# More products ahead of one head's last values and of another's third scores, and one unit's sums of weights tied behind the unit's addition

## The chip, the cores and the metric

The kernel runs on one core of one Trainium2 chip. Its time is the device time of one execution in microseconds, and lower is better. Three executions of the kernel before took 969.65, 969.67 and 970.43 us.

The profile's names for the engines are PE (TensorE's matmuls), PEld (TensorE's weight loads, which overlap the matmuls), DVE (VectorE), ACT (ScalarE), POOL (GpSimd) and SP (SyncE, which issues the loads of weights here).

## The reference, cut to what matters

The program is a decoder trunk of two layers over 512 tokens and 16 learned meta tokens, 1024 wide: first a gated linear attention, then a differential softmax attention with eight heads. All that the change touches lies in the second layer, and in that layer's projections:

```python
def diff_branch(xn, w_in, lam_vecs, gnorm, w_out, rel_table, lambda_init):
    proj = xn @ w_in
    q, k, v, z = jnp.split(proj, 4, axis=-1)
    ...
        s = jnp.einsum('bhpqd,bhpkd->bhpqk', qb, kh) * scale + bias[None, :, None]
        s = jnp.where(dist >= 0, s, -jnp.inf)
        p = jax.nn.softmax(s, axis=-1)
        a = p[:, :, 0] - lam * p[:, :, 1]
        return jnp.einsum('bhqk,bhkv->bhqv', a, vh)
    ...
    o = head_rms(o) * gnorm.astype(f32) * (1.0 - lambda_init)
    y = jax.nn.silu(z.astype(f32)) * o.reshape(B, L, D_INNER)
    return (y.astype(xn.dtype) @ w_out)
```

A head has two maps of scores, whose softmaxes are subtracted (`a`), values of 256 columns, a normalisation over them, a gate z, and its share of the output product.

## The kernel before, in words

**Exactness.** Every float32 operand of a matmul is split into a high and a low part (`split`, lines 284 and 285: ScalarE writes the high part, VectorE subtracts it from the source for the low part). A product is the sum of three matmul passes: high times high, high times low, low times high. In the profile `wh` and `wl` are the two parts of a block of weights, `a11h` and `a11l` those of one block, `aT` a head's turned weights of attention.

**Projections.** q, k, v and z of each head come from blocks of 256 columns of `w_in`. Each is a `Unit`: seven products of blocks instead of eight, with sums of weight blocks made ahead of them (`want_unit`, its function `sums` with three additions on VectorE, line 375; its block of raw weights comes by DMA, tile `raw`, and the sums go to the tile `sum`) and combinations of results after them (`add` in `Unit.run`, lines 493 to 497, which leaves its last instruction in `W.mark`). The banks of results are `bx`, `by` and `bv`. The q of heads 0 and 1 is a plain product of 512 columns instead (line 430, in `project`). A unit's column is its `c0`: q of head hd has c0 = 256 hd, so c0 = 768 is the q of head 3, whose weights are prepared while head 2 runs.

**What sets the order.** TensorE's instructions go in the order in which the program writes them. `W` (a `Weaver`) holds a queue of projections for the next head; between two steps of a head's attention, `W.fill(us)` takes so many microseconds of products off the queue, by a table of costs, and writes them there. VectorE's and ScalarE's instructions are ordered by a scheduler that knows priorities and dependences; `issue_after(x)` ties what stands in it behind the instruction x.

**A head's attention** (`diff_steps`) runs over four blocks of queries, the largest first. A step A makes the scores and the exponentials of a block (matmuls line 409, `ps<-k,q`; the shortest rows and sums on VectorE, line 1733; the exponential on ScalarE, line 1735), B turns the weights (lines 1757 and 1758, tiles `aT` and `am`), C makes the values (matmuls line 409, `ps<-v,aT`, and one short matmul, line 1773, `ps<-vm,am`) and normalises them: ScalarE, lines 1777 and 1778, a power on GpSimd, line 1780, and ScalarE again, line 1781, tile `on`. E turns two normalised blocks (line 1789, `ps<-ident,on`) and multiplies by z (VectorE, line 1792). The order of the steps with the number of the block is

```python
steps = [(A, 0), (A, 1), (B, 0), (A, 2), (C, 0), (B, 1), (A, 3), (C, 1), (B, 2), (E, 1), (C, 2), (B, 3),
         (C, 3), (E, 3)]
steps = [(f, o[i]) for f, i in steps]
```

with o = (3, 2, 1, 0), so `(C, 3)` makes the values of block 0. After each step stands a fill, whose least size depends on the step: 0 after A, 2.4 after B and C, 1.0 after E.

**The last head** keeps only the first six steps. The rest is written out after the loop, mixed with `final_rows`, the closing product with `w_out` (line 1863, `bx<-x,hT`). In this head lines 891 and 892 turn blocks of v (tiles `y` and `vm`; on VectorE lines 285 and 421), and lines 1589 to 1591 make the gate z.

Of the kernel before, what the change touches and what calls it, by code (L numbers as in the profile page):

```python
# [217 lines left out]
def trunk(ctx, tc, x, meta, g_norm, gla_w_in, gla_w_gate_up, gla_b_gate, gla_gnorm, gla_w_out,  # L218
# [9 lines left out]
    d_w_in, d_lam, d_gn, d_w_out = diff_w_in[0], diff_lam[0], diff_gnorm[0], diff_w_out[0]  # L228
# [85 lines left out]
    def in_rows(t):  # L314
        return t.rearrange("p (k c) -> p k c", c=P)
# [49 lines left out]
    def want_unit(w, c0, calm=False):  # L365
        def single(tag, b):
            def fn(raw):
                t = [T(wp, [P, 512], F32R, tag + part, bufs=1) for part in "hl"]
                with tc.issue_after(W.moved.ins) if calm and b == 0 else ExitStack():
                    split(*[in_rows(o) for o in t], block(raw, b))  # L370
                return t
            return Part(tag, fn)

        def add(o, a, b):
            dve.tensor_tensor(o, a, b, op=ALU.add)

        def sums(raw):
            t = T(wp, [P, 2, 512], F32, "sum", bufs=1)
            add(in_rows(t[:, 1, :]), block(raw, 2), block(raw, 3))
            add(in_rows(t[:, 0, :]), in_rows(t[:, 1, :]), block(raw, 0))  # L380
            add(block(raw, 2), block(raw, 2), block(raw, 0))
            return t

        def outer(raw):
            add(block(raw, 0), block(raw, 1), in_rows(su.t[:, 0, :]))
            ws.room["sum"] += 1
            return block_pair(raw[:, :4, :])

        a11, a12, a22 = single("a11", 0), single("a12", 1), single("a22", 3)
        su = Part("sum", sums)  # L390
        s21 = Part("pair", lambda raw: block_pair(su.t))
        s43 = Part("pair", outer)
        ws.want((w, c0), [a11, su, s21, a12, s43, a22])
        return a11, a12, a22, s21, s43
# [1510 lines left out]
    for hd in range(D_HEADS):  # L1905
        last = hd == D_HEADS - 1
        s = heads[hd]
        W.finish(projs[hd])
        W.settle()
        for chain in ready:  # L1910
            W.follow(*chain)
        ready.clear()
        s.scored, s.begun = False, True
        out2 = None
        keep = {D_HEADS - 1: 0.0, D_HEADS - 2: 22.0}.get(hd, 3.0)
        if 2 <= hd < D_HEADS - 1:
            pair = hd - 2 - hd % 2
            out2 = q_diff_out2(pair, ys[pair:pair + 2], range(2) if hd == D_HEADS - 2 else [hd % 2])
        if not last:
            n = heads[hd + 1]  # L1920
            late = hd == D_HEADS - 2
            if not late:
                gates.append(q_diff_z(hd + 1, n))
                values.append(q_diff_v(hd + 1, n))
            W.stop = q_diff_k(hd + 1, n)
            projs.append(q_diff_q(hd + 1, n))
            if late:
                values.append(q_diff_v(hd + 1, n))
                gates.append(q_diff_z(hd + 1, n))
        if hd == D_HEADS - 2:  # L1930
            ws.room["none"] = 0
            wt = want_last(hd)

            def freed():
                ws.room["none"] += 2
                ws.pump()
            gates[-1].freed = freed
        (A, B, C, E), o = diff_steps(hd, s, ys), (3, 2, 1, 0)
# [3 lines that stand above are left out]
        share = {A: 1.5, B: 1.1, C: 1.1, E: 0.5}  # L1942
        if last:
            steps = steps[:6]
        W.fill(4.0)
        for n, (f, b) in enumerate(steps):
            if last and n == 4:
                if values[hd] in W.queue:
                    W.finish(values[hd])
                W.settle()  # L1950
                W.fill(2.0)
            if n == 4:
                W.land()
            if n == 5 and gates[hd] in W.queue:
                W.finish(gates[hd])
            if last and n == 5:
                gfin = T(xp, [P, D], F32, "x0", bufs=1)
                sp.dma_start(gfin, g_final.partition_broadcast(P))
            if n == 5:
                if out2 in W.queue:  # L1960
                    W.finish(out2)
                ys.append([yt[hd % 3][:, i] for i in range(2)])
            f(b)
            if f is A and b == 0:
                s.scored, W.stop = True, None
                if not last:
                    heads[hd + 1].T = bias_tile(hd + 1)
            W.fill(max((W.left - keep) * share[f] / sum(share[g] for g, _ in steps[n:]),
                       ((4.0, 3.0, 5.2, 3.0, 4.6, 3.0, 4.0, 3.0)[hd]) if n == len(steps) - 2 else {A: 0.0, B: 2.4, C: 2.4, E: 1.0}[f]))
    W.finish()  # L1970
    W.settle()
    ws.pump()
# [53 lines left out]
```

## Time and profile before

| | |
|---|---|
| median of three runs | 969.67 us |
| profiled execution | 971.08 us |
| its span, first to last instruction | 968.4 us |
| mean granted TensorE clock | 0.996 |
| TensorE matmuls busy | 953.0 us, 98% of the span |
| VectorE busy | 798.2 us, 82% |
| ScalarE busy | 635.6 us, 66% |
| GpSimd busy | 81.3 us, 8% |

The first layer fills the span up to about 460 us. The first scores of head 0 stand at 501 us, those of head 1 at 555, of head 2 at 606, of head 3 at 668 and of the last head at 912. A row of the timeline gives start, busy time, engine, line, operation, tiles, and in brackets how long the engine had been idle and what released it. Several like instructions in a row are drawn together (x7), and their time is then the whole of it.

### The profile page before, as it was taken

To read this page: it belongs to the slowest core of one execution; us is meant where nothing else is said; L and a number is where in the kernel's file an instruction comes from. 1 tells how busy PE (TensorE), PEld (TensorE's weight loads), DVE (VectorE), ACT (ScalarE), POOL (GpSimd) and SP (SyncE) were. 2 spreads that over 40 slices of the span, in tenths; PEclk is the share of its full clock that TensorE was granted. 3 is DMA by queue.
4 is the path that set the end of the run, shared out by engine and by line. 5 is a ranking of instruction groups with operands and counts; after the bars stand their busy time and mean duration, and the time that the engine had idled before them with its cause. 6 is when DMAs were issued, how large, how long until landed. Compare 5 with 4: busy or idle time off the path is not lost.

```text
span 968.4 us, 18488 instructions
## 1 busy us (share of the span) xinstructions
PE 953.0 (98%) x7173; PEld 912.4 (94%) x7173; DVE 798.2 (82%) x1557; ACT 635.6 (66%) x1313; POOL 81.3 (8%) x164
## 2 busy tenths in 40 slices
PE   9999999999999999999999999999999999999997
PEld 8999999999999999998899898999999999989986
DVE  7989886886878787667997887879879889888875
ACT  7776755477647567656757685576766766755673
POOL 1000000000000000000001121111101101110111
PEclk9999999999999999999999999999999999999999
DMA  8322223635462237134356515234252261533312
GB/s 197 88 79 61 86 72 126 142 109 119 123 164 89 87 112 162 47 107 152 99 133 152 127 56 142 83 123 113 87 149 87 80 159 44 145 91 98 110 44 87
DMA packets 128602, 104.96 MB, mean 108 GB/s; under 512 B 51181, under 2 KB 112909, under 8 KB 128512
## 3 DMA queue, kind: packets, MB, share of 16 engines
q1 hardware_dynamic: 123184, 93.80, 35.3%
q10 hardware_dynamic: 5328, 9.95, 2.8%
q8 instruction: 57, 0.93, 0.4%
q14 instruction: 33, 0.27, 0.1%
HBM read 83.64 MB, written 11.80 MB: 99 GB/s over the span
## 4 chain that ended last, share of the span: by engine, by line
PE 73%; DVE 8%; ACT 4%; DMA 3%; issue 2%; POOL 1%; SPq 0%; POOLq 0%; DVEq 0%; ACTq 0%
PE bx L440 17%; PE bv L440 10%; PE by L440 9%; PE ps L409 7%; PE bx L997 5%; PE bx L430 4%; PE bx L409 3%; DMA raw<-in_diff_w_in_dram 3%; PE bv L997 2%; PE by L997 2%; PE ps L1239 2%; PE bv L409 1%; PE by L409 1%; DVE wl L285 1%; PE ps L1863 1%
## 5 line engine op out<-in xcount | busy, mean ns | idle before, releaser
L285 DVE TENSOR_TENSOR wl<-raw,wh 128x1024 fp32r<-128x1024 f32 x93 | 113.5, 1221 | 20.5 <-ACT wh L284 20.0
L284 ACT ACTIVATE wh<-raw 128x1024 fp32r<-128x1024 f32 x93 | 97.9, 1053 | 45.2 <-PE by L997 23.2
L440 PE MATMUL bv<-x,wh 128*128 128x264 f32 (+1 forms) x736 | 108.9, 285 | 0.1
L440 PE MATMUL bx<-x,wh 128*128 128x264 f32 (+1 forms) x720 | 105.6, 285 | 0.4 <-ACT ps L1777 0.4
L440 PEld LDWEIGHTS bv<-x,wh 128*128 128x128 f32 x736 | 96.8, 188 | 0.9 <-DVE z L497 0.3
L440 PEld LDWEIGHTS bx<-x,wh 128*128 128x128 f32 x720 | 94.4, 188 | 1.1 <-ACT ps L1777 0.7
L285 DVE TENSOR_TENSOR wl<-sum,wh 128x1024 fp32r<-128x1024 f32 x46 | 56.2, 1221 | 11.6 <-ACT wh L284 11.2
L461 ACT ACTIVATE u<-bx 128x264 f32<-128x264 f32 (+1 forms) x128 | 48.4, 378 | 21.8 <-PE bx L440 18.9
L440 PE MATMUL bv<-x,wl 128*128 128x264 f32 (+1 forms) x368 | 62.2, 286 | 0.1
L1735 ACT ACTIVATE p<-p,st 128x528 f32<-128x528 f32 (+3 forms) x64 | 36.4, 569 | 38.7 <-DVE st L1733 38.5
L440 PE MATMUL bx<-x,wl 128*128 128x264 f32 (+1 forms) x360 | 59.2, 284 | 0.0
L284 ACT ACTIVATE wh<-sum 128x1024 fp32r<-128x1024 f32 x46 | 48.4, 1051 | 10.4 <-PE bv L440 6.3
L440 PE MATMUL by<-x,a12h 128*128 128x264 f32 (+1 forms) x360 | 52.6, 285 | 0.9 <-DVE t L495 0.9
L440 PE MATMUL bx<-x,a11h 128*128 128x264 f32 (+1 forms) x360 | 53.0, 285 | 0.0
L440 PEld LDWEIGHTS bv<-x,wl 128*128 128x128 f32 x368 | 51.4, 188 | 0.4 <-issue 0.3
L284 ACT ACTIVATE a11h<-raw 128x512 fp32r<-128x512 f32 x46 | 28.9, 627 | 33.3 <-DMA raw<-in_diff_w_in_dram 12.8
L440 PEld LDWEIGHTS bx<-x,wl 128*128 128x128 f32 x360 | 50.0, 188 | 0.6 <-DVE wl L285 0.4
L440 PEld LDWEIGHTS bx<-x,a11h 128*128 128x128 f32 x360 | 47.8, 189 | 0.6
L440 PEld LDWEIGHTS by<-x,a12h 128*128 128x128 f32 x360 | 46.9, 188 | 1.1 <-DVE t L495 1.1
L565 POOL TENSOR_TENSOR st<-st,mhalf 128x1 f32<-128x1 f32 (+1 forms) x20 | 12.1, 606 | 386.5 <-DVE st L564 386.5
L1738 POOL TENSOR_TENSOR st<-st,minus 128x1 f32<-128x1 f32 x32 | 21.1, 658 | 279.4 <-ACT p L1735 226.4
L440 PE MATMUL by<-x,a22h 128*128 128x264 f32 (+1 forms) x280 | 40.1, 284 | 0.0
(501 smaller groups left out, 2671.8 us busy)
## 6 DMA issues: line engine op xcount, KB each, us to landing
raw<-in_diff_w_in_dram SPq DMA_DIRECT2D x52, 512.0 KB, 5.0
raw<-in_gla_w_in_dram SPq DMA_DIRECT2D x48, 512.0 KB, 4.5
raw<-in_gla_w_out_dram SPq DMA_DIRECT2D x8, 1024.0 KB, 6.0
raw<-in_diff_w_out_dram SPq DMA_DIRECT2D x8, 1024.0 KB, 5.3
raw<-in_diff_w_in_dram SPq DMA_DIRECT2D x6, 1024.0 KB, 6.0
vd<-planes ACTq DMA_DIRECT2D x12, 268.0 KB, 4.3
vd<-keep ACTq DMA_DIRECT2D x12, 264.0 KB, 2.3
T<-bdr SPq DMA_DIRECT2D x8, 264.0 KB, 3.8
```

Source lines behind the costliest of these rows:

```text
L284: act.activation(hi, src, AF.Copy)
L285: dve.tensor_tensor(lo, src, hi.bitcast(F32), op=ALU.subtract)
L409: pe.matmul(ps, l, r, start=first and n == 0, stop=last and n == 2, **kw)
L430: pe.matmul(bank, a[:, k, :], b[k] if n0 is None else b[k][:, n0 + i * nn:n0 + (i + 1) * nn], start=n == 0 and ks[0] == 0, stop=n == len(t ...
L440: pe.matmul(bank[:, :x[q].shape[2]], w[p][:, k * P:(k + 1) * P], x[q][:, k, :], start=first and i == 0, stop=i == len(PASSES) - 1, skip_gr ...
L461: W.moved = act.activation(t, self.bx[:, :self.n], AF.Copy, scale=self.sc)
L565: pool.tensor_tensor(dst, dst, mhalf[:np_, :dst.shape[1]], op=ALU.pow)
L997: pe.matmul(banks[i][:, :HT], h.t[p][:, k, mm * P:(mm + 1) * P], s.y[q][k][:, i * HT:(i + 1) * HT], start=n == 0, stop=n == len(PASSES) - 1)
L1239: pe.matmul(o, s.kd[:, i, kc], s.qs[:, i, t0:t0 + n], start=i == 0, stop=i == 1)
L1735: act.activation(p[:, :nk], p[:, :nk], AF.Exp, scale=-1.0, bias=st[:, m:m + 1], accum_out=st[:, 2 + m:3 + m])
L1738: pool.tensor_tensor(st[:, 5:6], st[:, 3:4], minus, op=ALU.pow)
L1863: pe.matmul(ps[i], yp[hd][p][:, k, b * P:(b + 1) * P], wt[q][cs.start // 512][:, 2 * hd + k, cs.start % 512:(cs.stop - 1) % 512 + 1], star ...
```

## The change

It has three parts. After the turn of block 0 in head 0 (step 11) the least fill is 5.2 instead of 2.4. In the last head a fill of 1.3 stands ahead of step 3, the scores of its third block. And the first addition of `sums` is tied behind `W.mark`, the latest addition of the unit that is running, for the unit with c0 = 768. The other two come behind it in any case: the second reads its sum, and the third overwrites a block that it reads.

```diff
         def sums(raw):
             t = T(wp, [P, 2, 512], F32, "sum", bufs=1)
-            add(in_rows(t[:, 1, :]), block(raw, 2), block(raw, 3))
+            with tc.issue_after(W.mark.ins) if (w is d_w_in and c0 in (768,)) else ExitStack():
+                add(in_rows(t[:, 1, :]), block(raw, 2), block(raw, 3))
             add(in_rows(t[:, 0, :]), in_rows(t[:, 1, :]), block(raw, 0))
             add(block(raw, 2), block(raw, 2), block(raw, 0))
             return t
...
                 W.settle()
                 W.fill(2.0)
+            if last and n == 3:
+                W.fill(1.3)
             if n == 4:
                 W.land()
...
             W.fill(max((W.left - keep) * share[f] / sum(share[g] for g, _ in steps[n:]),
-                       ((4.0, 3.0, 5.2, 3.0, 4.6, 3.0, 4.0, 3.0)[hd]) if n == len(steps) - 2 else {A: 0.0, B: 2.4, C: 2.4, E: 1.0}[f]))
+                       ((4.0, 3.0, 5.2, 3.0, 4.6, 3.0, 4.0, 3.0)[hd]) if n == len(steps) - 2 else {A: 0.0, B: 2.4 if hd or n < 11 else 5.2, C: 2.4, E: 1.0}[f]))
```

What this does to the order of instructions is seen on TensorE and VectorE. Lines of the new kernel are one higher from line 379 on, and three higher near its end. A row gives the line, the operation, result and operands with numbers that tell tiles of one name apart, and the shape.

TensorE in head 0, at its last values, before (seven products on wh stand at the sixth row, of which the first is shown):

```order
L430 MATMUL bx_9632<-x_1514_8558,wh_9560 128x512
L409 MATMUL ps_9642<-v_1525_8729,aT_1685_9618 128x256
L409 MATMUL ps_9642<-v_1526_8730,aT_1685_9618 128x256
L409 MATMUL ps_9642<-v_1525_8729,aT_1686_9619 128x256
L1773 MATMUL ps_9642<-vm_8731,am_9617 128x256
L430 MATMUL bx_9632<-x_1515_8559,wh_9560 128x512
L430 MATMUL bx_9632<-x_1512_8556,wl_9561 128x512 x4
L430 MATMUL bx_9632<-x_1514_8558,wl_9561 128x512 x4
L1789 MATMUL ps_9669<-ident,on_9647 128x128
L1789 MATMUL ps_9669<-ident,on_9596 128x128
L440 MATMUL bx_9692<-x_1512_8556,a11h_9688 128x256
```

The same place in the changed kernel, from the last product on wh:

```order
L431 MATMUL bx_9632<-x_1515_8559,wh_9560 128x512
L431 MATMUL bx_9632<-x_1512_8556,wl_9561 128x512 x4
L431 MATMUL bx_9632<-x_1514_8558,wl_9561 128x512 x4
L410 MATMUL ps_9657<-v_1525_8729,aT_1685_9618 128x256
L410 MATMUL ps_9657<-v_1526_8730,aT_1685_9618 128x256
L410 MATMUL ps_9657<-v_1525_8729,aT_1686_9619 128x256
L1774 MATMUL ps_9657<-vm_8731,am_9617 128x256
L1790 MATMUL ps_9669<-ident,on_9662 128x128
L1790 MATMUL ps_9669<-ident,on_9596 128x128
L441 MATMUL bx_9692<-x_1512_8556,a11h_9688 128x256
```

All 15 products of the queue (7 on wh, 8 on wl) now stand ahead of the values, and the transposes, whose first operand is `on` of these values, follow the values directly.

TensorE in the last head, from the turn of v to the values of the first block, before (of the six products of the third scores the first of each map is shown, of the values the first and the short one, of eight products on by with a12h the first):

```order
L892 MATMUL ps_14675<-ident,t_14485 32x128
L409 MATMUL ps_14688<-k_2557_14148,q_2594_14333 128x272
L409 MATMUL ps_14695<-k_2557_14148,q_2594_14333 128x272
L440 MATMUL bv_14670<-x_1540_8784,wh_14501 128x256 x5
L440 MATMUL bv_14670<-x_1540_8784,wl_14502 128x256 x4
L440 MATMUL bx_14719<-x_1542_8786,wh_14630 128x256 x8
L440 MATMUL bx_14719<-x_1542_8786,wl_14631 128x256 x4
L440 MATMUL bx_14738<-x_1543_8787,a22h_14634 128x256 x8
L440 MATMUL bx_14738<-x_1543_8787,a22l_14635 128x256 x4
L409 MATMUL ps_14751<-y_2654_14645,aT_2647_14613 128x256 x2
L1773 MATMUL ps_14751<-vm_14646,am_14612 128x256
L440 MATMUL by_14775<-x_1514_8558,a12h_14505 128x256
```

The same in the changed kernel:

```order
L893 MATMUL ps_14675<-ident,t_14485 32x128
L441 MATMUL bv_14670<-x_1540_8784,wh_14501 128x256 x5
L441 MATMUL bv_14670<-x_1540_8784,wl_14502 128x256 x4
L441 MATMUL bx_14701<-x_1542_8786,wh_14630 128x256 x3
L410 MATMUL ps_14707<-k_2557_14148,q_2594_14333 128x272
L410 MATMUL ps_14714<-k_2557_14148,q_2594_14333 128x272
L441 MATMUL bx_14701<-x_1542_8786,wh_14630 128x256 x5
L441 MATMUL bx_14701<-x_1542_8786,wl_14631 128x256 x4
L441 MATMUL bx_14737<-x_1543_8787,a22h_14634 128x256 x8
L441 MATMUL bx_14737<-x_1543_8787,a22l_14635 128x256 x4
L441 MATMUL by_14756<-x_1514_8558,a12h_14505 128x256
L410 MATMUL ps_14769<-y_2654_14645,aT_2647_14613 128x256 x2
```

Twelve products (nine on bv, three on bx) have moved ahead of the scores, and the twelve on by (eight with a12h, four with a12l), which stood behind the values, now stand ahead of them.

VectorE in head 2, where the tie works, before:

```order
L375 TENSOR_TENSOR sum_10952<-raw_10762 128x512
L375 TENSOR_TENSOR sum_10952<-sum_10952,raw_10762 128x512
L375 TENSOR_TENSOR raw_10762<-raw_10762 128x4x128
L285 TENSOR_TENSOR a11l_10949<-raw_10762,a11h_10948 128x512
L375 TENSOR_TENSOR raw_10762<-raw_10762,sum_10952 128x4x128
L495 SCALAR_TENSOR_TENSOR t_10825<-by_10895,u_10861 128x264
L285 TENSOR_TENSOR a22l_10945<-raw_10579,a22h_10944 128x512
```

And in the changed kernel (of the rows between, three that have not moved against each other are left out):

```order
L285 TENSOR_TENSOR a11l_10949<-raw_10762,a11h_10948 128x512
L496 SCALAR_TENSOR_TENSOR t_10825<-by_10895,u_10861 128x264
L285 TENSOR_TENSOR a22l_10945<-raw_10579,a22h_10944 128x512
L375 TENSOR_TENSOR sum_10952<-raw_10762 128x512
L375 TENSOR_TENSOR sum_10952<-sum_10952,raw_10762 128x512
L285 TENSOR_TENSOR wl_10941<-raw_10579,wh_10940 128x1024
L375 TENSOR_TENSOR raw_10762<-raw_10762 128x4x128
L375 TENSOR_TENSOR raw_10762<-raw_10762,sum_10952 128x4x128
```

The first two additions of `sums` have gone behind the addition t and the split a22l, the third and the one that follows from them behind the split wl. The fourth, last row is the addition of `outer`, which needs the sum.

## The prediction

> **What bounds the kernel now.** I read the page's head, its busy times and its chain of waits first.
>
> ```profile
> span 968.4 us, 18488 instructions
> PE 953.0 (98%) x7173; PEld 912.4 (94%) x7173; DVE 798.2 (82%) x1557; ACT 635.6 (66%) x1313; POOL 81.3 (8%) x164
> PE 73%; DVE 8%; ACT 4%; DMA 3%; issue 2%; POOL 1%; SPq 0%; POOLq 0%; DVEq 0%; ACTq 0%
> ```
>
> TensorE is busy for 98% of the span, and the chain runs through it for 73%. No matmul is added or removed, so only TensorE's idle time can change. The profiled execution took 971.08 us, 2.7 us more than its span of 968.4; the runs' median is 969.67. A difference of span is carried to that median as it is. The second view is the list of waits of the weight loads (engine, line, waited for: us in total, times, longest us).
>
> ```profile
> PEld ps L409 <- DVE vm L421: 1.4, 1, 1.4
> PEld ps L409 <- ACT aT L284: 1.3, 1, 1.3
> PEld by L440 <- DVE t L495: 1.1, 1, 1.1
> ```
>
> The second row stands in front of the first head's last values (545 us), the first in front of the last head's third scores (924 us): where the two fills are put. The third lies at 707 us in head 3. The tie works at 640 us, in head 2, and not on it.
>
> **Head 0: 15 products ahead of the values.** The timeline around it (start, us, engine, line, operation, count, and in brackets the idle time before and who ended it):
>
> ```profile
> 541.89 1.63 POOL L1780 TENSOR_TENSOR st<-st,mhalf 128x1 f32<-128x1 f32 x1 [8.88 <-ACT on L1778]
> 541.89 1.22 DVE L285 TENSOR_TENSOR wl<-raw,wh 128x1024 fp32r<-128x1024 f32 x1
> 542.11 2.25 PE L430 MATMUL bx<-x,wh 128*128 128x512 f32 x9
> 545.19 0.51 PEld L409 LDWEIGHTS ps<-v,aT 128*128 128x128 f32 x3 [1.26 <-ACT aT L284]
> 545.58 0.60 ACT L287 ACTIVATE q<-bx 128x512 fp32r<-128x512 f32 x1
> 545.92 0.39 PE L1773 MATMUL ps<-vm,am 96*128 96x256 f32 x1
> 546.15 1.80 PE L430 MATMUL bx<-x,wh 128*128 128x512 f32 x7
> 546.35 0.17 ACT L1777 ACTIVATE ps<-st 128x1 f32<-128x1 f32 x1 [0.17 <-PE ps L1773]
> 547.11 0.55 POOL L1780 TENSOR_TENSOR st<-st,mhalf 128x1 f32<-128x1 f32 x1 [3.59 <-ACT on L1778]
> 547.69 0.47 ACT L1781 ACTIVATE on<-ps,st 128x256 f32<-128x256 f32 x1 [0.66 <-POOL st L1780]
> 547.78 2.02 PE L430 MATMUL bx<-x,wl 128*128 128x512 f32 x8
> 548.61 0.69 DVE L375 TENSOR_TENSOR sum<-raw 128x512 f32<-128x512 f32 x1 [0.89 <-DMA raw<-in_diff_w_in_dram]
> 549.34 0.69 DVE L375 TENSOR_TENSOR sum<-sum,raw 128x512 f32<-128x512 f32 x1
> 549.41 0.59 PEld L1789 LDWEIGHTS ps<-ident,on 128*128 128x128 f32 x4
> 550.00 1.19 PE L440 MATMUL bx<-x,a11h 128*128 128x256 f32 x8
> ```
>
> One product of 512 columns takes (547.78 − 546.15)/7 = 0.233 us. After the nine at 542.11 the next could begin at 542.11 + 9 × 0.233 = 544.20. Instead the values wait for aT until 545.19, and products go on at 546.15. The values' own work is some 0.5 us of this (three of 0.12 and the short one), so the wait costs about 1.47 us. That is what the fill aims at.
>
> With the change, 15 products run in it, from 544.20 to 544.20 + 15 × 0.233 = 547.69. The values begin at 547.69, long after aT. This stall is gone. But the queue of products is now empty: the next row on TensorE is the transposes L1789, whose first operand is the result of these very values. Before, the same 15 products stood between the two, from 546.15 to 549.80 (547.78 + 2.02), and covered the whole chain values → L1777, L1778 → GpSimd L1780 → L1781. That chain took from the end of the short product, 545.92 + 0.39 = 546.31, to 547.69 + 0.47 = 548.16, which is 1.85 us. It now starts when the short product ends: 547.69 + 0.36 (three values) + 0.28 (the short one, without today's wait inside its 0.39) = 548.33, and ends at about 550.2. The transposes' weights are loaded from 550.25 instead of 549.41, 0.84 later; before, that load ran ahead of a TensorE still busy with products, so some 0.1 of it doesn't count. **Head 0: +0.75 us, a loss.** The stall of 1.47 us becomes one of about 2.2 us at the next instruction.
>
> Lower end: if ScalarE goes through L1777 and L1778 without the second half of q (a copy like the 0.60 us one at 545.58, ready at the same moment) between, +0.6. Upper end: the GpSimd step. At 541.89 it took 1.63 us instead of 0.55, and ended 0.41 us after VectorE's subtraction wl (541.89 + 1.22 = 543.11), which has two inputs in SBUF. In the new order it arrives at about 549.15, while VectorE adds the sums (548.61 to 550.03, two such adds). If it has to wait for both, it ends at 550.03 + 0.41 = 550.44 instead of 549.7: +1.5. I take +0.75, since the first add ends at 549.30, and 549.30 + 0.41 = 549.71 is no later than 549.15 + 0.55.
>
> [...]
>
> Is a shift here carried to the end? From 550 to 706 us no weight load waits for more than 0.3 us, and VectorE is nearly full in head 1 (the window, its us, then busy PE, PEld, DVE, ACT, POOL, the granted clock, DMA share, GB/s):
>
> ```profile
> 559.00:566.00 7.00, 7.00 (x58) 6.99 (x57) 6.61 (x15) 5.36 (x13) 2.71 (x6) 1.00 0.00 0
> 566.00:573.00 7.00, 7.00 (x60) 7.00 (x60) 6.76 (x15) 5.99 (x15) 1.66 (x3) 1.00 0.51 151
> ```
>
> So nothing is taken back there, and VectorE, left with 0.39 and 0.24 us of air in 7, may add up to 0.3 us if it falls further behind than TensorE. The wait at 707 us could take some back, if the load that the sums wait for at 703 us doesn't move:
>
> ```profile
> 703.24 0.69 DVE L375 TENSOR_TENSOR sum<-raw 128x512 f32<-128x512 f32 x1 [0.77 <-DMA raw<-in_diff_w_in_dram]
> 706.98 0.78 PEld L440 LDWEIGHTS by<-x,a12h 128*128 128x128 f32 x6 [1.06 <-DVE t L495]
> ```
>
> Its buffer is freed by work that follows TensorE, so I put that at nothing, and between 0 and −0.75 for the range.
>
> **Head 2: the tie.** Three adds of the unit of q of head 3 (two make the sums, one changes the raw block) move behind the addition t:
>
> ```profile
> 639.50 0.68 DVE L375 TENSOR_TENSOR sum<-raw 128x512 f32<-128x512 f32 x1
> 642.76 0.42 DVE L495 SCALAR_TENSOR_TENSOR t<-by,u 128x264 f32<-128x264 f32 x1
> 649.47 1.22 DVE L285 TENSOR_TENSOR wl<-sum,wh 128x1024 fp32r<-128x1024 f32 x1 [0.27 <-ACT wh L284]
> ```
>
> Nothing on TensorE waits for that addition here, so nothing is saved. VectorE idles about 1 us near 640.5, since t waits for TensorE, and 2 us of adds have to be fitted in between 643 and 649. What needs them is wl at 649.47, which waits for ScalarE by 0.27 us today. **0 us.** Bounds: 0 and +1.0, if all the idle time comes out at that wl and TensorE waits for it.
>
> **Tail: 12 products ahead of the third scores.**
>
> ```profile
> 922.70 0.10 PEld L892 LDWEIGHTS ps<-ident,t 128*32 128x32 f32 x1
> 923.80 0.37 SPq L293 DMA_DIRECT2D raw<-in_diff_w_out_dram  x1
> 924.19 0.43 PEld L409 LDWEIGHTS ps<-k,q 128*128 128x128 f32 x3 [1.39 <-DVE vm L421]
> 925.28 0.67 PEld L440 LDWEIGHTS bv<-x,wh 128*128 128x128 f32 x5
> 926.36 1.01 PEld L440 LDWEIGHTS bx<-x,wh 128*128 128x128 f32 x8
> 928.14 3.04 ACT L284 ACTIVATE x<-raw 128x1024 fp32r<-128x1024 f32 x3
> 932.90 0.55 POOL L1780 TENSOR_TENSOR st<-st,mhalf 128x1 f32<-128x1 f32 x1 [3.59 <-ACT on L1778]
> 933.03 0.68 DVE L1591 SCALAR_TENSOR_TENSOR z<-z,t 128x512 f32<-128x512 f32 x1
> 933.63 1.22 DVE L285 TENSOR_TENSOR x<-raw,x 128x1024 fp32r<-128x1024 f32 x1
> 936.64 0.69 DVE L1591 SCALAR_TENSOR_TENSOR z<-z,t 128x512 f32<-128x512 f32 x1 [0.68 <-ACT t L1590]
> 937.90 0.42 ACT L284 ACTIVATE hT<-yt 128x256 fp32r<-128x256 f32 x1 [1.29 <-DVE yt L1792]
> 939.16 1.01 PEld L1863 LDWEIGHTS bx<-x,hT 128*128 128x128 f32 x5
> ```
>
> The weight loads could go on at 922.80 and wait until 924.19. The 12 products (nine on bv, three on bx, 0.12 us each by the eight at 926.36) fill 922.80 to 924.22, and the scores run up to 925.28 as before. Product four on bx is at 925.28 instead of 926.72: **1.44 us gained at this place.**
>
> What then ends last before the closing products L1863 (939.16)? ScalarE's copies of the last weights (928.14, three) hang on the load issued at 923.80, which I take not to move, and on(3) comes behind them as before: values(3) are 1.44 earlier by the gain and 12 × 0.12 = 1.44 later, because the 12 products on by have moved ahead of them. So the GpSimd step stays near 932.9. If it gets in before the last subtraction x, which can now start at about 933.0, then x ends at 934.25, the last z follows (TensorE's bv is 1.44 earlier, VectorE's addition behind x 0.5 earlier), and L1863 starts at about 938.0: −1.1. If x goes first, as a subtraction of 1.22 us did at 541.89, GpSimd ends at 934.66, ScalarE's queue (on, aT, am, z) is that much later, and L1863 begins at about 939.0: −0.15. I take the middle of the two with the gain at the scores as the far end: **−0.8 us, between −0.1 and −1.44.**
>
> **Sum:** +0.75 + 0 − 0.8 = −0.05 us: 969.67 − 0.05 = 969.6.
>
> **Rivals.**
>
> A. *Both waits are saved.* −1.47 − 1.44 = −2.9: 966.8. For it: the two rows are the longest waits on the list. Against: L1789 needs on from the values directly ahead, and the chain's 1.85 us has nothing in front of it any more.
>
> B. *GpSimd behind VectorE, slower.* In head 0 the step waits for both adds (+1.5), VectorE in head 1, with 0.24 us of air, adds 0.3, and in the tail x goes first and on comes later than today (+0.2): +2.0, 971.7. It decides where L1780 starts at 549.15: above about 550.4 for its end, this is the case. For it: 1.63 us at 541.89. Against: three things have to come out badly.
>
> C. *The tie costs.* wl<-sum late by 1 us and TensorE behind it: +1.0 − 0.05, 970.6. For it, 0.27 us of air on ScalarE; against, that VectorE has 6 us to catch up.
>
> That the change does nothing is held by the forecast's time too (969.7), but the order of TensorE's instructions speaks against it: only the sum is near nothing, not its parts.
>
> **How the numbers follow.** Forecast 0.66, A 0.16, B 0.13, C 0.05. What a measurement can tell from no change is about 0.2%, 1.9 us. The forecast's own range is +0.6 − 1.44 = −0.85 (−1.6 with the wait at 707) to +1.5 − 0.1 = +1.4: 968.1 to 971.1. Half of A and half of B stay outside 967.6 to 971.3. Faster by over 0.2% is A and the forecast's lowest corner, 0.16 + 0.03 = 0.19; slower is B, 0.13; the rest 0.68.
>
> **What would show it.** In the profile after: no wait ahead of the values near 548 us, and a wait of 1.7 to 2.7 us of L1789's weight load for ScalarE's on near 550. No weight load near 924 that waits over 0.3 us, and L1863's second part 0.1 to 1.4 us earlier against the scores. No wait of TensorE in 640 to 652. The prediction is wrong if L1789 starts without a wait, if the stall at 707 grows or goes, or if VectorE's lag after 550 shows as a new wait in head 1.

## The result: slower by 4 us, and the profile after

The changed kernel takes 974.54 us (median of seven runs, 973.02 to 976.85), the kernel before 970.34 in the same comparison. The ratio is 1.0046, with a 95% interval of 1.0035 to 1.0057: slower, by 3.4 to 5.5 us. The forecast was no change, 969.6 with a range up to 971.3. The runs after also spread over 3.8 us.

The profiled execution has a span of 971.5 us, 3.1 more than before, with TensorE as busy as before (953.2 us). Three rows of its list of waits of the weight loads (engine, line, waited for: us in total, times, longest us; the rows between them, of the first layer and of L1778, are left out):

```profile
PEld ps L1790 <- ACT on L1782: 2.6, 1, 2.6
PEld ps L410 <- issue: 1.8, 1, 1.8
PEld by L441 <- DVE t L496: 1.0, 1, 1.0
```

The two waits that the fills aim at (1.3 and 1.4 us before) are gone from the list. Two others are now its longest single waits: the transposes of head 0, right behind the values, and the values of block 1 in the last head (L410). The third, in head 3, is nearly as it was (1.1 before, 1.0 now).

The timeline of the changed kernel at the first place (start, us, engine, line, operation, and in brackets the idle time before and who ended it):

```profile
547.10 0.54 PEld L410 LDWEIGHTS ps<-v,aT 128*128 128x128 f32 x3
548.72 0.69 DVE L375 TENSOR_TENSOR sum<-sum,raw 128x512 f32<-128x512 f32 x1
548.78 1.04 POOL L1781 TENSOR_TENSOR st<-st,mhalf 128x1 f32<-128x1 f32 x1 [5.84 <-ACT on L1779]
549.86 0.47 ACT L1782 ACTIVATE on<-ps,st 128x256 f32<-128x256 f32 x1 [1.15 <-POOL st L1781]
550.38 0.42 PEld L1790 LDWEIGHTS ps<-ident,on 128*128 128x128 f32 x4 [2.62 <-ACT on L1782]
550.79 2.01 PE L441 MATMUL bx<-x,a11h 128*128 128x256 f32 x8
553.69 0.39 ACT L462 ACTIVATE u<-bx 128x256 f32<-128x256 f32 x1
```

The values run without a wait, as forecast. GpSimd's power takes 1.04 us beside the addition that started 0.06 us earlier, and ends 0.41 us after it. The weight load of the transposes waits 2.62 us; the matmuls themselves stand still for 2.42, since the last of the loads ended 0.20 us ahead of the short product (547.76 against 547.96). And then something that the forecast did not have: the eight products behind the wait take 2.01 us, where the same eight took 1.19 before. The windows of the profile say why (the window, its us, busy PE, PEld, DVE, ACT, POOL, the granted clock, DMA share, GB/s):

```profile
547.44:550.85 3.41, 0.99 (x10) 0.79 (x8) 2.82 (x4) 1.61 (x5) 1.04 (x1) 1.00 0.01 2
550.85:554.27 3.42, 3.42 (x18) 3.42 (x17) 2.73 (x6) 1.82 (x4) 0.00 (x0) 0.50 0.56 154
```

From 550.86 to 554.27, for 3.41 us, TensorE was granted half its clock (0.50).

At the second place, in the last head:

```profile
926.75 0.44 PEld L410 LDWEIGHTS ps<-k,q 128*128 128x128 f32 x3
935.39 1.22 DVE L285 TENSOR_TENSOR x<-raw,x 128x1024 fp32r<-128x1024 f32 x1
935.39 1.62 POOL L1781 TENSOR_TENSOR st<-st,mhalf 128x1 f32<-128x1 f32 x1 [3.28 <-ACT on L1779]
937.05 0.47 ACT L1782 ACTIVATE on<-ps,st 128x256 f32<-128x256 f32 x1 [1.74 <-POOL st L1781]
939.77 0.69 DVE L1592 SCALAR_TENSOR_TENSOR z<-z,t 128x512 f32<-128x512 f32 x1 [0.95 <-ACT t L1591]
941.10 1.14 PEld L410 LDWEIGHTS ps<-y,aT 128*128 128x128 f32 x9 [1.80 <-issue]
941.13 1.31 PE L410 MATMUL ps<-y,aT 128*128 128x256 f32 x9 [1.69 <-DVE yt L1793]
942.28 1.24 PEld L1864 LDWEIGHTS bx<-x,hT 128*128 128x128 f32 x6
```

The scores no longer wait, but GpSimd's power starts in the same 10 ns as VectorE's subtraction x and lasts 1.62 us instead of 0.55. ScalarE's on, aT, am and z follow it, and TensorE stands still for 1.69 us (its weight loads for 1.80) ahead of the values of block 1, until VectorE's yt is done.

How far TensorE stands behind the kernel before (differences of the start of the same matmul in the two timelines):

| place | before, us | after, us | shift |
|---|---|---|---|
| short product of block 1, head 0 (L1773) | 538.28 | 537.93 | −0.35 |
| transposes of blocks 0 and 1, head 0 (L1789) | 549.65 | 550.38 | +0.73 |
| first short product of head 1 | 572.58 | 574.89 | +2.31 |
| head 3, short product of its last block | 717.97 | 720.18 | +2.21 |
| last head, its first short product | 930.75 | 933.25 | +2.50 |
| last head, turn of block 1 (L1757) | 933.72 | 934.77 | +1.05 |
| last head, second short product | 939.16 | 942.28 | +3.12 |
| first of the last six closing products on bx (L1863) | 958.48 | 961.60 | +3.12 |

So head 0 costs 1.1 us up to the transposes and 1.6 us behind them; the heads between 0.2; in the tail 1.45 us are gained at 934 and 2.1 lost at 942, together 0.6. That makes 3.5 us in this execution, from −0.35 to +3.12; the timed medians lie 4.2 us apart, and the other 0.7 is not placed.

The half clock alone explains neither the loss nor the spread. Of the seven timed runs one has a mean clock of 0.998 and a span of 971.2 us, five have 0.996 and 971.3 to 974.4, one has 0.994 and 972.3. The kernel before has a median span of 967.8 us in the runs beside part one below. So the changed kernel loses over 3 us in a run with a high clock too, and its runs with the same mean clock still lie 3 us apart. Why they do is open.

### The profile page after: what moved, and what is told of

Same layout as the page of the kernel before. It is cut to its first block, busy times and chain, and to the rows that moved or that the text cites. A ratio compares the mean times of both kernels' runs of the same rounds, so it can differ in the third digit from the quotient of the medians.

```text
span 971.5 us, 18483 instructions
## 1 busy us (share of the span) xinstructions
PE 953.2 (98%) x7173; PEld 912.7 (94%) x7173; DVE 798.5 (82%) x1557; ACT 636.1 (65%) x1313; POOL 83.8 (9%) x164
## 4 chain that ended last, share of the span: by engine, by line
PE 79%; DVE 4%; ACT 4%; DMA 2%; issue 1%; POOL 1%; POOLq 0%; SPq 0%; DVEq 0%; ACTq 0%
PE bx L441 19%; PE bv L441 12%; PE by L441 11%; PE ps L410 8%; PE bx L998 5%; PE bx L431 4%; PE bx L410 3%; PE by L998 2%; PE bv L998 2%; PE ps L1240 2%; PE bv L410 1%; PE by L410 1%; DMA raw<-in_diff_w_in_dram 1%; PE ps L1864 1%; PE bx L1864 1%
```

## The experiments

In each, spans of single runs are used beside the times: a run records its span and its mean granted clock.

**One part alone (three kernels).** The three edits of the change, each by itself, everything else as before.

Part one, the fill of 5.2 in head 0:

> Only the first part of the change: the larger fill after the turn of block 0 in head 0. Theory (half clock): the whole of what the changed kernel loses in its first 560 us comes back here. The transposes wait about 2.4 us for on, they start about 1.1 us later than before against the shift ahead of them, and the granted clock then stands at 0.5 for about 4 us, which costs 1.6 us more: span +2.7, time +2.5 to +3.0 us. Rival (the other engines): the stall alone is the loss, +1.1, and the rest of what is lost by 560 us comes from the tie's or the tail's part of the change; then this kernel is +1.0 to +1.3 slower.

Measured: 972.06 us against 969.78, ratio 1.0024 (1.0009 to 1.0038), a median of +2.3 between theory and rival. The profile shows less than the theory said, and a wait that it didn't have:

```profile
548.42 0.55 POOL L1780 TENSOR_TENSOR st<-st,mhalf 128x1 f32<-128x1 f32 x1 [5.82 <-ACT on L1778]
549.53 0.42 PEld L1789 LDWEIGHTS ps<-ident,on 128*128 128x128 f32 x4 [2.13 <-ACT on L1781]
549.94 1.20 PE L440 MATMUL bx<-x,a11h 128*128 128x256 f32 x8
552.13 0.63 ACT L284 ACTIVATE hT<-yt 128x512 fp32r<-128x512 f32 x1 [2.65 <-DVE tick L639]
553.70 1.01 PEld L440 LDWEIGHTS bx<-x,wh 128*128 128x128 f32 x8 [0.87 <-ACT u L461]
```

In this execution GpSimd started 0.05 us ahead of the addition (548.47) and took its 0.55 us; the weight load waited 2.13 us, the matmuls 1.92, and the clock stayed at 1.00: the eight products take 1.20. Up to the transposes the loss is 0.58 us (from −0.70 to −0.12 in the shift). Then another 0.98 us is lost: ScalarE's copy u comes behind hT in the new order, hT waits for VectorE's yt, and the products that write u's bank wait 0.87 us. From there to the last head another 0.5 us is lost in small pieces (+0.86 at 572 us, +1.36 at 931). In the changed kernel the same u was as late (553.69), but at half clock the products ahead of it were done no earlier: there the half clock takes the place of the wait for u, and the two do not add up. Two things, then: the stall that I forecast at the transposes, and a place in ScalarE's queue that I had not followed. VectorE's and ScalarE's orders in head 0 are those of the changed kernel. So of two executions of the same head 0 one has the half clock and the other has not.

Part three, the fill of 1.3 in the last head:

> Only the third part: the fill of 1.3 ahead of the third scores of the last head. Theory (GpSimd behind VectorE): the 1.4 us ahead of the scores are gained and lost again, since the power on GpSimd starts together with VectorE's second subtraction x and lasts 1.6 us instead of 0.55, and the aT, am and z of ScalarE's queue come behind it: the closing products start 0.6 us later than before, time +0.4 to +0.8 us. Rival (the load): the closing products hang on the load of the last weights, which does not move, and the gain is only hidden: 0, from -0.2 to +0.2. Rival (my forecast): -0.8.

Measured: 971.17 against 969.78, ratio 1.0012 (1.0002 to 1.0021), above the theory's 0.4 to 0.8. The power again meets x, the values of block 1 wait 1.69 us, and here the clock fell:

```profile
931.65 1.62 POOL L1780 TENSOR_TENSOR st<-st,mhalf 128x1 f32<-128x1 f32 x1 [3.12 <-ACT on L1778]
937.39 1.49 PE L409 MATMUL ps<-y,aT 128*128 128x256 f32 x9 [1.69 <-DVE yt L1792]
```

```profile
931.51:934.92 3.41, 3.35 (x18) 2.55 (x16) 2.38 (x5) 1.64 (x6) 1.62 (x1) 1.00 0.00 0
934.92:938.33 3.41, 1.72 (x14) 1.60 (x15) 2.09 (x8) 1.86 (x5) 0.15 (x1) 1.00 0.00 0
938.33:941.75 3.42, 3.42 (x12) 2.84 (x11) 0.47 (x4) 1.63 (x6) 1.33 (x4) 0.50 0.02 5
```

The ten runs fall into two groups: six with a mean clock of 0.996 or 0.997 and spans of 969.3 to 969.7 us, four with 0.998 and 967.8 to 968.9. The mean alone doesn't say where a run lost its clock: 6 of the 27 runs of the kernel before have 0.996 or 0.997 as well, and its profiled execution had 3.41 us at a clock of 0.50 at the program's start. The same wait of 1.69 us in the changed kernel, at 939.4, left the clock at 1.00.

Part two, the tie:

> Only the second part: the sums of q of head 3 tied behind the addition. Theory: nothing, since no weight load waits near 640 us; the shift of TensorE between 630 and 660 us changes by less than 0.1 us, and the time by -0.2 to +0.2 us. Rival (the tie costs): the changed kernel's additional 0.2 us between 560 and 900 us come from here, +0.2 to +1.0 us.

Measured: 969.46 against 969.78, ratio 0.9997 (0.9987 to 1.0007). The shift of TensorE is −0.94 at 572 us, −0.94 at 639 and −0.94 at 700: the tie in head 2 does nothing.

**Is it the half clock? Fill the wait.** In part three's trace the clock of 0.50 came behind TensorE's wait of 1.69 us. If it is the wait that brings it on, and if it is what splits part three's runs, work in the wait must join the groups, though the wait itself stays: both are assumptions that this run tries. This is part three with 15 transposes in the wait. ScalarE's order is part three's, VectorE's too but for two neighbours near 852 us.

```diff
+            if hd == D_HEADS - 1 and b == 2:
+                bank = pb_tile("by")
+                for _ in range(15):
+                    pe.transpose(bank[:, :P], R[3].on[:, :P], ident)
             ps = ps_tile()
             po = ps[:, :256]
```

> The third part alone, with 15 additional transposes of a block that is ready, into a bank that is read no more, ahead of the last head's values of block 1, where TensorE waited 1.69 us (VectorE's and ScalarE's orders are the same, instruction by instruction). The wait itself is not shortened: 15 x 0.11 = 1.65 us of it is filled. Theory (half clock): with the third part alone 6 of 10 runs had a granted clock of 0.996 to 0.997 and a span of 969.3 to 969.7 us, the other four 0.998 and 967.8 to 968.9. With the wait filled no stretch of half clock stands behind it, the runs lie at the lower group, 967.8 to 968.9 us, and the median falls by 0.8 to 1.5 us against the third part alone: within -0.3 to +0.5 us of the kernel before. Rival (the slow group has another cause, such as the start of the program): two groups in about the same numbers as before, median +1.2 us against the kernel before.

Measured: 969.90 against 969.44, ratio 1.0006 (0.9997 to 1.0016).

```profile
935.71 1.62 PEld L1771 LDWEIGHTS by<-ident,on 128*128 128x128 f32 x15
937.57 1.12 PEld L409 LDWEIGHTS ps<-y,aT 128*128 128x128 f32 x9 [0.24 <-issue]
```

The values start where they started (937.57 against 937.36), and the closing products keep the pace: between the second short product and the last closing products this execution loses nothing, where part three alone lost 1.4 us (its shift went from −0.48 to +0.95). Eight of ten runs lie at 967.4 to 968.6 with a clock of 0.998 or 0.999; two are left, 968.7 with 0.996 and 969.9 with 0.997, about the share that the kernel before has. Against the kernel before in the same comparison the median is +0.5 us where part three alone had +1.4, so the useless work takes off about 1 us; the two intervals overlap, so the totals alone don't prove it. That the clock was halved behind the wait is shown in part three's trace (0.50 from 938.34 us on), and its price there is 1.4 us; that filling the wait prevents it is not shown, and rests on the counts, 6 of 10 against 2 of 10, and on the next run's trace more than on this one: here the step of 3.41 us at the wait (by the estimate in the last section) has 3.16 us of busy TensorE, and still 2.00 without the transposes. What remains is the wait: +0.5 us in the median, with an interval that includes 0, and 0.8 us of the tail in this profile.

The same was tried in head 0, with 20 transposes ahead of the four that wait:

```diff
             pt = ps_tile()
+            if hd == 0 and rs[0].b == 0:
+                for _ in range(20):
+                    pe.transpose(pt[:, P:2 * P], rs[1].on[:, :P], ident)
```

> The first part of the change with 20 additional transposes of the block that is ready (into the bank that the four real ones fill afterwards, so the result is the same) between the values and the transposes that wait: TensorE has 2.1 us of work where it waited 1.9 to 2.4 us. Theory (half clock): what is lost over the moved stall is the granted clock, which fell to 0.5 for 3.4 us behind the wait in the changed kernel. Here no stretch of 0.5 stands between 540 and 560 us, and the loss is that of the moved stall alone: +0.6 to +1.2 us, also in the timed runs, and their spread is smaller than that of the first part alone (971.6 to 973.9 there). Rival (the stall alone, whatever TensorE does in it): as the first part alone, +2.3 us.

Measured: 976.01 against 969.79, ratio 1.0073 (1.0054 to 1.0091). No stretch of half clock stands in it ahead of the program's end, and up to 572 us the shift is +0.94, within 0.1 us of part one's whole-clock execution. Then the shift grows to +2.1 at 826 us, +2.6 at 835 and +4.1 at 930. The order of instructions is not the reason: VectorE's and ScalarE's are those of part one, but for one memset. Two loads of weights come late instead, and VectorE's first addition of the sums waits for them, 1.53 and 2.08 us where part one waited 0.53 and 0.50:

```profile
818.00 0.69 DVE L375 TENSOR_TENSOR sum<-raw 128x512 f32<-128x512 f32 x1 [1.53 <-DMA raw<-in_diff_w_in_dram]
907.44 0.69 DVE L375 TENSOR_TENSOR sum<-raw 128x512 f32<-128x512 f32 x1 [2.08 <-DMA raw<-in_diff_w_in_dram]
```

They were issued 0.2 and 1.1 us later than in part one, and their additions start 1.2 and 2.7 us later; why the loads take longer is open. So neither number is met, and the total says nothing about head 0. For the clock the trace does say something. The step from 547.15 to 550.56 us (3.41 us, placed by the estimate in the last section) has 3.31 us of busy TensorE, and 1.13 without the 20 transposes. Steps with 0.99 and 1.72 us were followed by half clock in the changed kernel and in part three; this one was not.

**How many products ahead.** The fill in head 0 decides how many products stand between the values and the transposes: 15 before, none with the change.

```diff
-                       ... B: 2.4 if hd or n < 11 else 5.2, ...
+                       ... B: 2.4 if hd or n < 11 else 3.6, ...
```

> The first part with a fill of 3.6 instead of 5.2: six products more than before stand ahead of the values (1.4 us), nine stay between the values and the transposes (2.1 us). Theory: both waits are covered. The values wait at most 0.2 us (aT was ready 0.99 us after TensorE), the chain to on takes 1.85 us, under the 2.1 us of products: no wait, no drop of the clock, -1.2 to -1.5 us. Rival (GpSimd behind VectorE here as well): its power meets a subtraction of 1.22 us, on comes up to 1.1 us later, the transposes wait about 0.9 us: -0.5 us.

Measured: 968.68 against 969.78, ratio 0.9994 (0.9984 to 1.0003). In the profile the shift goes from −0.61 to −1.71: 1.1 us gained, between theory and rival but close to the theory. The power takes its 0.55 us, and a rest of a wait is left, which the theory did not have:

```profile
547.68 0.42 PEld L1789 LDWEIGHTS ps<-ident,on 128*128 128x128 f32 x4 [0.42 <-ACT on L1781]
```

And with 4.6, twelve ahead and three behind, where ScalarE's u stands ahead of hT again:

> The first part with a fill of 4.6: twelve products more than before stand ahead of the last values of head 0, three between them and the transposes. Against the first part alone (15 and 0) ScalarE's order differs in one thing: the copy u of the next unit's first bank stands ahead of hT again, as before the change; there it stood behind hT and the first v, and TensorE waited 0.66 us more for it. Theory (two waits, the moved stall and u behind hT): the transposes wait about 1.2 us and start within 0.2 us of their old time against the shift ahead of them, u is not late, and nothing more is lost: time -0.3 to +0.4 us, and no stretch of half clock, since the wait is shorter than 1.5 us. Rival (the moved stall alone makes the loss of the first part, whatever ScalarE's order): +0.8 to +1.3 us.

Measured: 969.53 against 968.86, ratio 1.0009 (0.9999 to 1.0018).

```profile
548.90 0.42 PEld L1789 LDWEIGHTS ps<-ident,on 128*128 128x128 f32 x4 [1.82 <-ACT on L1781]
551.10 0.36 ACT L461 ACTIVATE u<-bx 128x256 f32<-128x256 f32 x1
552.13 1.01 PEld L440 LDWEIGHTS bx<-x,wh 128*128 128x128 f32 x8
```

The weight load of the transposes waits 1.82 us and the matmuls 1.39, against the 1.2 expected; u is there in time (no wait at 552.13), and the shift goes from −0.80 to −0.69: 0.1 us lost in the profiled execution, as the theory of two waits has it. Part one alone lost 1.56 there. Of the difference 0.5 us stands up to the transposes, where three products fewer are ahead, and 0.9 behind them, where u is no longer late. ScalarE's order differs in more than u (the next split a11h goes ahead too, and VectorE's order behind it changes), but u is what the products waited for in part one. The timed median is some 0.5 us above what the profile explains; the interval covers both. The eight products on a11h behind the wait take 1.20 us, as with a clock of 1.00 in part one. The bound of 1.5 us in the expectation was my estimate, and no run shows it: half clock stood behind a wait of 1.69 us in part three, and none behind 1.92 in part one.

**GpSimd behind VectorE.** In the tail, one small VectorE operation that reads the power's result keeps x behind it:

```diff
             pool.tensor_tensor(ms, ms, mhalf[:, :1], op=ALU.pow)
+            if hd == D_HEADS - 1 and r.b == 3:
+                dve.tensor_scalar(r.st[:, 7:8], ms, 1.0, 0.0, op0=ALU.mult, op1=ALU.add)
             act.activation(r.on, po, AF.Copy, scale=ms)
```

> The third part with one additional VectorE operation of 128x1 that reads the result of GpSimd's power of the last head's first values, so that the subtraction x comes behind it in VectorE's order. Theory (GpSimd behind VectorE): the power lasts 0.55 us instead of 1.62, on, aT, am and z come about 1 us earlier, the wait ahead of the values of block 1 falls from 1.7 to under 0.8 us, and the closing products start 0.4 to 1.0 us earlier than before the change against the shift ahead of them: -0.4 to -1.0 us. Rival (the load of the last weights): on comes earlier but the wait stays, since the last z hangs on ScalarE's copies of these weights: +0.4 to +1.2 us as with the third part alone.

Measured: 969.57 against 969.79, ratio 0.9999 (0.9989 to 1.0008).

```profile
932.58 0.55 POOL L1780 TENSOR_TENSOR st<-st,mhalf 128x1 f32<-128x1 f32 x1 [3.35 <-ACT on L1778]
934.50 0.99 PEld L1865 LDWEIGHTS ps<-x,hT 128*128 128x128 f32 x5 [0.83 <-DVE x L285]
937.58 1.12 PEld L409 LDWEIGHTS ps<-y,aT 128*128 128x128 f32 x9 [0.95 <-issue]
```

The power takes 0.55 us and the wait ahead of the values falls from 1.81 in part three to 0.95, but the held-back x now makes the closing products wait 0.83 us. The cause is right, the remedy moves the stall: the tail ends within 0.2 us of the kernel before, which is neither theory's number.

A remedy without a held operation: the next fill of the last head at 0.7 instead of 2.0, so that its first values stand ahead of the products on by again.

```diff
                 W.settle()
-                W.fill(2.0)
+                W.fill(0.7)
```

> The third part with a fill of 0.7 instead of 2.0 in the next step, so that the last head's first values stand ahead of the twelve products on by as before the change; only the twelve products ahead of the third scores are moved. Theory (GpSimd behind VectorE): the power's place among VectorE's subtractions decides. On ScalarE the copies of the last weights still stand ahead of on, so on comes no earlier than now, but both subtractions x stand ahead of z here and end before the power starts at about 932.9: it takes 0.55 us, -0.5 to -1.2 us. Rival (the load): 0, from -0.3 to +0.3. Rival (the power meets z, also with two inputs in SBUF): +0.3 to +1.0 us.

Measured: 968.92 against 969.79, ratio 0.9989 (0.9980 to 0.9999): 0.9 us faster than before in the median, between 0.1 and 1.9.

```profile
932.92 0.55 POOL L1780 TENSOR_TENSOR st<-st,mhalf 128x1 f32<-128x1 f32 x1 [3.04 <-ACT on L1778]
936.73 0.41 PEld L409 LDWEIGHTS ps<-k,q 128*128 128x128 f32 x3 [0.46 <-DVE am L419]
```

Both x lie ahead of the power, and only 0.46 us of wait is left. With the six products of head 0 beside it:

> Six products ahead in head 0 (fill 3.6) and the third part with the values ahead of the products on by, no tie: the sum of the two. Theory: -1.1 (head 0, as its own run's profile shows) and -0.5 to -1.2: -1.6 to -2.3 us. Rival (one of the two gains is lost again behind it): -0.5 to -1.1 us.

Measured: 967.92 against 969.79, ratio 0.9979 (0.9969 to 0.9988). That is −1.9 us, against −1.1 and −0.9 for the two alone: within the interval they add up.

**The tie where a wait is.** Last, the tie on the unit with c0 = 1024 instead of 768, on top of that kernel:

> Six products ahead in head 0, the third part with the values first, and the tie on the unit with c0 = 1024 (the q of head 4, made ready in head 3), where TensorE did wait for an addition behind the sums, 1.0 us. Theory: the addition t leaves VectorE's queue ahead of the sums, the wait near 706 us falls under 0.3 us, and what comes off that unit's sums later has 6 us: 0.7 to 1.0 us better than the same kernel without the tie, so -2.7 to -3.0 us against the kernel before. Rival (the sums come late instead): the wait comes back at the products on the sums' halves, and the time is that of the kernel without the tie, -2.0 us.

Measured: 964.97 against 968.86, ratio 0.9962 (0.9951 to 0.9974): 3.9 us faster than before (2.5 to 4.7), in the median more than the theory's 3.0.

```profile
700.53 0.43 DVE L496 SCALAR_TENSOR_TENSOR t<-by,u 128x264 f32<-128x264 f32 x1
701.71 0.68 DVE L375 TENSOR_TENSOR sum<-raw 128x512 f32<-128x512 f32 x1
703.47 0.79 PEld L441 LDWEIGHTS by<-x,a12h 128*128 128x128 f32 x6
```

The addition is done ahead of the sums, and the weight load that waited 1.06 us before waits for nothing. The wait of 0.7 us for L1777 five microseconds later, which the theory did not count, went with it: the shift goes from −2.38 at 698 us to −4.54 at 713. ScalarE's copies ahead of that L1777 start earlier here as well; that they had stood behind the same additions is likely but not shown. This is the fastest of all kernels here, and beats the kernel before and the change.

## Why the prediction was wrong, step by step

- **The sum.** It had three terms and took what lies between them as nothing: head 0 +0.75, tie 0, tail −0.8. In the changed kernel's profile they are +1.1 up to the transposes, +1.6 behind them, 0.2 in the heads between, which hold the tie, and +0.6 in the tail. The two errors of the forecast are the missing +1.6 and the sign of the tail.
- **Head 0, the stall that moves: the mechanism was right.** The values start at 547.10, the transposes wait 2.62 us, and the power is as late as the upper bound said: it started 0.06 us behind the second addition and ended 0.41 us after it. Part one's profile shows the other outcome, 0.55 us, with a lead of 0.05 us. Both outcomes were in the prediction; the value taken (+0.75) is near the +0.58 to the transposes in that one, and the changed kernel shows +1.08, inside the +0.6 to +1.5 given. Between the two lies some 0.1 us (0.05 ahead of an addition, 0.06 behind its start), so that part of the range was rightly left open. In these rows the power takes 1.04 us where it starts behind the start of an addition, 1.62 where it starts with a subtraction of 1.22 us, and 0.55 where it starts ahead of the addition. The prediction's upper end asked whether it has to wait for both additions. In the kernel before, at 815 us, it did not: it starts inside the first of two additions and ends 0.42 us after that first one, while the second runs:

```profile
815.41 0.69 DVE L375 TENSOR_TENSOR sum<-raw 128x512 f32<-128x512 f32 x1 [0.48 <-DMA raw<-in_diff_w_in_dram]
815.61 0.91 POOL L1780 TENSOR_TENSOR st<-st,mhalf 128x1 f32<-128x1 f32 x1 [3.29 <-ACT on L1778]
816.14 0.69 DVE L375 TENSOR_TENSOR sum<-sum,raw 128x512 f32<-128x512 f32 x1
```

- **Head 0, behind the stall: this step failed.** It is "From 550 to 706 us no weight load waits for more than 0.3 us", with "So nothing is taken back there": a reading of the trace of before, carried over to the changed order, which put the loss behind the stall at nothing but VectorE's 0.3. The runs show 1.0 us there in part one and 1.6 in the changed kernel. With a whole clock it is ScalarE's queue: u behind hT, 0.87 us of wait in part one, and no wait in the run with twelve products ahead, where u stands ahead of hT. The edit's order on ScalarE was there to be read, and I priced TensorE's queue alone. With the half clock it is 3.41 us at a clock of 0.50, in the changed kernel's profile. The prediction gave the new wait its length and no consequence.
- **Tail: the mechanism was right, the choice in the middle was not.** The prediction had a case in which x goes first, with "L1863 begins at about 939.0: −0.15", and one at −1.1, and took −0.8. In the changed kernel and in part three alone, x and the power start together and the power takes 1.62 us instead of 0.55; in the run with 0.7 instead of 2.0, where both x lie ahead of the power, the tail is faster than before. The size of that case was off as well: not −0.15 but +0.6 us, and its 939.0 was not worked out from rows. The last z starts 0.6 us later than before against the shift ahead of it, yt follows it, and TensorE stands still at the values of block 1 until yt is done. They write a bank of results and read nothing of yt's, so it is taken to be the bank that yt reads. Where the half clock follows, as in part three's trace, another 1.4 us is lost there; the median of part three's runs is +1.4.
- **Tie: right.** Nothing waits there, and nothing changed.
- **The range.** Rival B named GpSimd behind VectorE in both places as the slower case and priced it at +2.0; the measured +4.2 is outside it by what follows the stall in head 0, and by a tail of +0.6 instead of +0.2. Summed over the parts alone, 1.0024 + 1.0012 − 0.0003 give 1.0033, against 1.0046 (1.0035 to 1.0057) for the whole; the intervals overlap, and 1.3 us is left unexplained or is chance. Of the changed kernel's two waits the one of 2.42 us had half clock behind it and the one of 1.69 us had not, but only one of its executions has a trace, and the mean clocks of its runs do not sort their spans.

## What to carry to other kernels

Filling a wait with work that stood behind it takes that work away from the next wait: count what is left between the moved step and the first instruction that reads its result, and move only as much as the first wait needs (six products gained 1.1 us, fifteen lost 1.6). Then follow each engine's queue past the place, not only TensorE's, and put a tie where the list of waits has a row. On a TensorE that is busy for 98% of the span a wait of 1.69 us cost nearly twice its length in part three's profile: the clock stood at 0.50 for 3.41 us behind it, which cost 1.4 us more. In the changed kernel's profile a wait of the same length had a clock of 1.00 behind it.

## What the runs showed of the hardware that I had not expected

**A wait of 1.69 us had half the clock behind it.** By the granted clock in windows of 0.25 us, it fell from 1.00 to 0.50 at 8.29 and 964.02 us in the execution before (the second after the last matmul), at 550.86 and 967.28 in the changed kernel, at 938.34 and 965.64 in part three. Each halving during the work lasted 3.41 us. The two falls of an execution lie 955.73, 416.42 and 27.30 us apart, which is 280, 122 and 8 times 3.413. From these three distances I estimate that the clock of these executions changes at steps of 3.41 us; nothing but these distances shows it. Laid out by this estimate, the step ahead of the fall had 0.99 us (head 0, changed kernel) and 1.72 us (tail, part three) of busy TensorE. In the changed kernel's tail the same wait of 1.69 us falls across two steps:

```profile
936.56:939.97 3.41, 2.71 (x15) 1.96 (x14) 1.43 (x5) 2.61 (x6) 0.46 (x1) 1.00 0.00 0
939.97:943.39 3.42, 2.26 (x15) 2.12 (x16) 1.94 (x8) 1.91 (x8) 0.97 (x4) 1.00 0.02 5
```

They have 2.71 and 2.26 us, and the clock stays at 1.00. In part one's execution a wait of 1.92 us leaves 2.02 and 2.89 us, and it stays as well; with twelve products ahead the step at the wait of 1.39 us has 2.02 us, and it stays. Where 20 transposes filled the wait in head 0, a step with 1.13 us of other work has 3.31 in all, and it stays. By the same estimate a step begins 1.46 us after the first instruction in the execution before and 3.08 us after it in part three, so the same wait can fall inside one step or across two. At the start of the program the busy time of a step does not sort the executions: the one before lost its clock there after a step with 2.31 us of busy TensorE (4.88 to 8.29 us), and the one of the changed kernel kept it with 2.27 (4.73 to 8.14). So the runs show which waits had half clock behind them, 2.42 and 1.69 us, and which had not, 1.69, 1.92 and 1.39 us; what decides it they do not show.
